# Giving VectorE's remainders of Q and K, the rounded parts' products and the adaLN columns another place in a hybrid attention layer's order of work

## The chip, the cores and the metric

The kernel runs on one core of a Trainium2 chip. The metric is the device time of one execution in microseconds, the lower the better. All matrix products are made in a rounded 32-bit type (float32r) with every operand split in two: a rounded part and the remainder that the rounding left. A product of two such operands takes three passes (rounded by rounded, rounded by remainder, remainder by rounded).

## The reference, cut to what matters

One layer of a streaming encoder is computed for 1024 rows of a prompt and 64 rows of a sample, with 1024 cached rows for the sample. `h` is a normalized and modulated `x` whose shift, scale and gate come from a product with `w_ada` (adaLN). Then:

```python
m = jax.nn.silu(c) @ w_ada[l] + b_ada[l]                  # shift1, scale1, gate1, shift2, scale2, gate2
qd, kd, vd, qs, ks, vs = split_proj(pre(h, g_pre_mix, shift1, scale1) @ w_in[l])
p = jax.nn.softmax(jnp.where(visible, qd kd^T * scale - alibi, NEG))       # 4 heads, two maps each
od = rmsnorm((p[0] - lam * p[1]) @ vd, subln_g) * (1 - lam_init)
w = jnp.where(earlier, jnp.exp(log_sigmoid(z) + between), 0)               # 8 heads, stick-breaking
osb = w @ vs
h = h + gate1 * rmsnorm(concat(od, osb) @ w_out, g_post_mix)
h = h + gate2 * rmsnorm(relu(pre(h, g_pre_ffn, shift2, scale2) @ w_up) ** 2 @ w_down, g_post_ffn)
```

K and V of both groups of heads are outputs too.

## The kernel before, in words

The head of the kernel loads a part of `w_ada`, turns its product into columns (A1, B1) and makes the transposed, split activations `hT` in three groups of columns (384, 384, and 256 of the prompt plus 64 of the sample). Then come eight units of 128 columns of Q, K and V: units 0 to 3 are the heads of differential attention, units 4 to 7 hold two stick-breaking heads each. After them come `w_out` and the second norm, and then the FFN in 16 blocks.

In the middle part two streams of work are written into each other. The main stream is a list of steps (`Diff`, `Stick`, `Sample`), each with `score` (products with K, exponentials or sigmoids) and `apply` (transposes, products with V). The second stream is a `Filler`: a first-in, first-out list of generators, in which each `yield` gives a cost. After each `yield` of the main stream, `fill.spend` runs the filler's generators until their costs have paid for the main stream's cost times a ratio, and `fill.until` drains what a step needs at once. The filler holds `proj(u, g)` for unit u and group g (in the order `proj_q`, `proj_k`, `proj_v`) at a cost of 12 each, and from unit 2 on one part of `rows` (the rows of gate1, then `modulation`, whose `ada_rows` and columns A2 and B2 the second norm needs).

`proj_q` makes 24 products of one PSUM bank `pq` (tag `pj`, two banks for all of the filler's work). Then, for each half of 64 partitions, ScalarE writes the rounded scaled copy (L488) and VectorE the remainder (L489), so that they are written as copy, remainder, copy, remainder. `proj_k` does it with one whole copy `kf` and two rounded copies in each half (L512, L513), and a remainder (L514). It then transposes `kf` and stores it (`natural`).

`apply` works in groups of up to four blocks of 128 by 128. A group is transposed into a PSUM bank, ScalarE rounds it (`ah`), VectorE takes the remainder (`al`, L65), and one group later `times` makes the products with V: for each block one with `ah` and one with `al` (L620 and L621 for Diff and Sample, L788 and L789 for Stick). All of a step's products add up in one bank `po`.

In `modulation`, VectorE copies the product's bank to `R` (L224), and two products with `sel` sum it into columns (L209). In the trace these tiles carry the names `Rm` and `pcm`.

The build plans the engines' orders itself: `TileContext(nc, schedule_with_timeline_sim=True)` is given the written order, and what the engines run is not the written order line for line. Semaphores are placed by it too. The engines are in order once it is built.

Of the kernel before, what the change touches and what calls it, by code (L numbers as in the profile page):

```python
# [16 lines left out]
P = 128  # L17
# [13 lines left out]
def fr(ap):  # L31
    return ap.bitcast(F32)


def build(tc, I, O):
# [17 lines left out]
    def brief(shape, name, tag, dt=F32, bufs=2):  # L53
        return atp.tile(shape, dt, tag=tag, name=name, bufs=bufs)

    def bank(name, tag):
        return pp.tile([P, 512], F32, tag=tag, name=name)

    load = nc.sync.dma_start
    mm = nc.tensor.matmul  # L60
# [60 lines left out]
    cc = brief([16, P], "cc", "o1", bufs=1)  # L121
# [83 lines left out]
    def sum_to_columns(R, n, name):  # L205

        ps = bank(name, "pj")
        for i in range(n):
            mm(ps[:, 2 * i : 2 * i + 2], lhsT=R[:, i * P : (i + 1) * P], rhs=sel, start=True, stop=True)  # L209
        return ps[:, 0 : 2 * n].rearrange("p (k j) -> p k j", j=2)  # L210

    def modulation(first, cols, name):

        A, B = (sb.tile([P, KT, 2], F32, name=x + name) for x in "AB")

        def gen():
            for q in range(4):
                ks = slice(2 * q, 2 * q + 2)
                for part in range(2):
                    nm = f"{name}{q}{part}"  # L220
                    c0 = first + D * part + 256 * q
                    ps = yield from ada_rows(c0, nm)
                    R = big("R" + nm, "s", [P, 512], F32)[:, :256]
                    nc.vector.tensor_copy(R, ps)  # L224
                    v = sum_to_columns(R, 2, "pc" + nm)
                    col = lambda c: cols[:, c : c + 2].unsqueeze(2).broadcast_to([P, 2, 2])
                    o = (B, A)[part][:, ks, :]
                    nc.vector.tensor_tensor(o, v, col(8 + (c0 - first) // P), ALU.add)
                    if part:
                        nc.vector.scalar_tensor_tensor(o, o, 1.0, col(2 * q), ALU.add, ALU.mult)  # L230
                    yield None

        return A, B, gen()
# [240 lines left out]
    def proj_q(u, g, wq):  # L474
        c0, n = GRP[g]
        qs = -0.125 if u < 4 else 0.125
        if g == 0:
            U[u]["Q"] = [big(f"Q{u}{m}", "qk", [P, TP]) for m in range(2)]
        Q = U[u]["Q"]
        if u + g:  # L480
            ps = bank(f"pq{u}{g}", "pj")
            yield from dense_T(ps, wq, hT, g)
        else:
            ps = PS[0]
        w = min(n, TP - c0)
        for m in range(2):
            r, o = slice(64 * m, 64 * m + 64), slice(64 - 64 * m, 128 - 64 * m)
            nc.scalar.mul(Q[m][r, c0 : c0 + w], ps[r, :w], qs)  # L488
            nc.vector.scalar_tensor_tensor(Q[m][o, c0 : c0 + w], ps[r, :w], qs, fr(Q[m][r, c0 : c0 + w]), ALU.mult, ALU.subtract)  # L489
        if g == 2:  # L490
            qsm = brief([P, TS], f"qsm{u}", "ms", bufs=1)
            nc.scalar.mul(qsm, ps[:, 256:320], qs)
            load(smD[u, :, 0, :], qsm)

    def proj_k(u, g, wk):
        c0, n = GRP[g]
        if g == 0:
            U[u]["Kd"] = [big(f"K{u}{m}", "qk", [P, TP]) for m in range(2)]
            U[u]["Kl"] = big(f"Kl{u}", "qk", [P, TP])
        Kd, Kl = U[u]["Kd"], U[u]["Kl"]  # L500
        if u + g:
            ps = bank(f"pk{u}{g}", "pj")
            yield from dense_T(ps, wk, hT, g)
        else:
            ps = PS[1]
        w = min(n, TP - c0)
        cols = slice(c0, c0 + w)
        kf = small([P, 384], f"kf{u}{g}", "kf", bufs=2)
        nc.scalar.copy(kf[:, :n], ps[:, :n])
        for m in range(2):  # L510
            r, o = slice(64 * m, 64 * m + 64), slice(64 - 64 * m, 128 - 64 * m)
            nc.scalar.copy(Kd[m][r, cols], ps[r, :w])  # L512
            nc.scalar.copy(Kd[m][o, cols], ps[r, :w])  # L513
            nc.vector.tensor_tensor(Kl[r, cols], ps[r, :w], fr(Kd[m][r, cols]), ALU.subtract)  # L514
        if g == 2:
            load(smD[u, :, 1, :], kf[:, 256:320])
        natural(kf, u, g, kout, f"k{u}{g}")
        yield 0.33
# [91 lines left out]
    def apply_rows(po, parts, values):  # L610

        n = sum(len(p[0]) for p in parts)
        done = 0
        pend = []

        def times(ah, al, blocks, kr):
            nonlocal done
            for i in range(len(blocks)):
                v = values(done)
                mm(po[:, 0:256], lhsT=ah[:kr, i * P : (i + 1) * P], rhs=v.rearrange("p a d -> p (a d)"), start=(done == 0), stop=False, skip_group_check=True)  # L620
                mm(po[:, 0:P], lhsT=al[:kr, i * P : (i + 1) * P], rhs=v[:, 0, :], start=False, stop=(done == n - 1), skip_group_check=True)  # L621
                done += 1

        for blocks, kr, name, pre in parts:
            if pre:
                pre()
            pend.append((*transposed(blocks, name, kr), blocks, kr))
            yield 0.11 * len(blocks)
            if len(pend) == 2:
                times(*pend.pop(0))  # L630
                yield 0.8
        yield 0.1
        while pend:
            times(*pend.pop(0))
            yield 0.8
# [111 lines left out]
    class Stick:  # L747
# [26 lines left out]
        def apply(self):  # L774
            u, q, hd = self.u, self.q, self.hd
            r, o = slice(64 * hd, 64 * hd + 64), slice(64 - 64 * hd, 128 - 64 * hd)
            V = U[u]["V"]
            po = bank(f"po{self.name}", "pv")
            pend = []

            def times(jp, ah, al):
                for i in range(2):
                    j = 2 * jp + i
                    v = V[:, j, hd, :]
                    lone = j == 2 * q + 1
                    out = po[:, P:256] if lone else po[:, 0:256]
                    cc = slice(256, 384) if lone else slice(256 * i, 256 * i + 256)
                    mm(out, lhsT=v, rhs=ah[:, cc], start=(j == 2 * q), stop=False, skip_group_check=True)  # L788
                    mm(out, lhsT=v, rhs=al[:, cc], start=False, stop=(j == 1), skip_group_check=True)  # L789

            for jp in reversed(range(q + 1)):
                blocks = [(j, t) for j in (2 * jp, 2 * jp + 1) for t in range(2) if not (j == 2 * q + 1 and t == 0)]
# [290 lines left out]
    for m in range(NTT):  # L1083
        g, off = m // 3, (m % 3) * P
# [28 lines left out]
        r = rstd(sumsq([p[:rows] for p in pss], rows, f"sso{m}", jk), rows, f"rso{m}")  # L1113
# [3 lines left out]
        r = rstd(sumsq([a[:rows] for a in x], rows, f"ssb{m}", jk), rows, f"rsb{m}")  # L1117
# [114 lines left out]
    for b in range(NB - 1):  # L1232
# [12 lines left out]
        if last:  # L1245
            GG2 = gate("g2", 1, "h")
            wd2 = [down_weights(b + 1, i, i == 0) for i in range(2)]
            done = []
# [57 lines left out]
```

## Time and profile before

| | us |
|---|---|
| median of 3 runs | 1553.53 (1546.62 to 1556.1) |
| the profiled execution's own time | 1554.56 |
| its span, from first to last instruction | 1552.7 |
| busy in the span: TensorE, its weight loads | 1499.0, 1341.8 |
| busy in the span: VectorE, ScalarE, GpSimd | 918.1, 700.1, 342.7 |

The span is cut below into the head (to 75 us), the eight units (75 to 600 us), the turn from the last unit to `w_out` (600 to 690 us), and the rest (from 690 us). A busy TensorE is not TensorE at its peak, since matmuls overlap and their ends are modelled; the distance from one matmul's start to the next tells its rate. In a view of waits a line reads: the waiting engine, its tile and line, who ended the wait, the total in us, the number of times, the longest.

### The profile page before, as it was taken

What the parts mean: (1) busy time and instruction counts of PE and PEld (TensorE: products, weight loads), DVE (VectorE), ACT (ScalarE), POOL (GpSimd) and SP (SyncE); (2) the same over time, 40 slices, a digit from 0 to 9 for tenths busy, and PEclk for the clock granted to TensorE, in tenths of its full rate; (3) what the DMA queues carried; (4) which work ended last, traced back from release to release, by engine and by line L of the source; (5) the groups of instructions that cost most, each with busy time, mean ns of one, the idle gap of its engine ahead of it and who ended that gap; (6) DMA issues with size and microseconds to landing.
All of it is one profiled execution on the core that took longest, in us unless ns stands there. A gap on an engine that the chain in (4) does not pass through costs nothing.

```text
span 1552.7 us, 23586 instructions
## 1 busy us (share of the span) xinstructions
PE 1499.0 (97%) x8714; PEld 1341.8 (86%) x8714; DVE 918.1 (59%) x1761; ACT 700.1 (45%) x1650; POOL 342.7 (22%) x519
## 2 busy tenths in 40 slices
PE   6899999989999999899999999999999999999998
PEld 4789898878899988778898988899989999899896
DVE  3776877675868687866442445454554544544447
ACT  3766766666768577837653112121122112121122
POOL 1453443434333333622110000000000000000002
PEclk9999999999999999999999999999999999999999
DMA  9322333424232325444221122211111111111025
GB/s 315 119 60 82 93 115 100 119 62 124 71 113 60 111 88 159 124 122 140 75 66 52 34 79 82 70 40 41 55 54 41 46 37 42 54 55 41 28 82 183
DMA packets 152517, 133.20 MB, mean 86 GB/s; under 512 B 11234, under 2 KB 136275, under 8 KB 152403
## 3 DMA queue, kind: packets, MB, share of 16 engines
q1 hardware_dynamic: 152402, 131.71, 27.6%
q8 instruction: 68, 1.11, 0.3%
q14 instruction: 47, 0.38, 0.1%
HBM read 108.59 MB, written 23.09 MB: 85 GB/s over the span
## 4 chain that ended last, share of the span: by engine, by line
PE 64%; issue 4%; ACT 4%; DVE 3%; POOL 1%; DMA 1%; SPq 0%; DVEq 0%; POOLq 0%; ACTq 0%
PE pu L303 8%; PE pu L305 8%; PE pu L304 8%; PE pd L1181 8%; PE pd L1182 8%; PE pd L1184 7%; PE py L1096 1%; PE py L1098 1%; PE pt L604 1%; PE py L1095 1%; PE po L789 1%; PE pq L303 1%; PE pq L305 1%; PE pq L304 1%; PE pk L303 1%
## 5 line engine op out<-in xcount | busy, mean ns | idle before, releaser
L1188 DVE TENSOR_TENSOR acc<-pd,acc 128x512 f32<-128x512 f32 x252 | 171.8, 687 | 113.6 <-PE pd L1184 107.8
L1166 ACT ACTIVATE sq<-pu 128x384 f32<-128x384 f32 (+1 forms) x96 | 45.1, 470 | 308.3 <-PE pu L305 308.3
L1167 DVE TENSOR_TENSOR sq<-sq 128x384 f32<-128x384 f32 (+1 forms) x96 | 72.1, 751 | 171.8 <-ACT sq L1166 171.8
L65 DVE TENSOR_TENSOR al<-pt,ah 128x512 fp32r<-128x512 f32 (+2 forms) x128 | 75.6, 598 | 19.1 <-ACT ah L64 17.7
L593 PE MATMUL pz<-K,Q 128*128 128x128 f32 (+2 forms) x192 | 72.9, 382 | 4.5 <-DVE mn L678 1.9
L64 ACT CAST ah<-pt 128x512 fp32r<-128x512 f32 (+2 forms) x128 | 65.9, 522 | 24.5 <-PE pt L604 16.7
L604 PE MATMUL pt<-ident,s 128*128 128x128 f32 x432 | 70.0, 277 | 4.2 <-DVE al L65 1.5
L642 ACT ACTIVATE s<-s,mn 128x512 f32<-128x512 f32 (+3 forms) x96 | 58.6, 611 | 23.3 <-DVE mn L678 19.7
L594 PE MATMUL pz<-Kl,qz 128*128 128x128 f32 (+2 forms) x192 | 66.6, 350 | 0.0
L740 DVE TENSOR_TENSOR_SCAN s<-k,s 128x128 f32<-128x128 f32 (+1 forms) x64 | 58.2, 922 | 11.4 <-POOL s L769 7.1
L604 PEld LDWEIGHTS pt<-ident,s 128*128 128x128 f32 x432 | 51.6, 141 | 9.2 <-DVE al L65 2.0
L65 DVE TENSOR_TENSOR rl<-sq,rh 128x384 fp32r<-128x384 f32 x64 | 35.7, 558 | 38.1 <-ACT rh L64 38.1
L442 POOL CAST qz<-Q 64x256 fp32r<-64x256 f32 x64 | 36.9, 576 | 90.5 <-PE pz L594 71.8
L764 ACT ACTIVATE s<-pz 128x128 f32<-128x128 f32 (+2 forms) x96 | 47.8, 498 | 15.5 <-PE pz L594 14.9
L64 ACT CAST rh<-sq 128x384 fp32r<-128x384 f32 x64 | 32.8, 513 | 40.2 <-DVE sq L1167 38.2
L765 ACT ACTIVATE k<-pz 128x128 f32<-128x128 f32 (+2 forms) x96 | 47.9, 499 | 0.0
L789 PE MATMUL po<-al,V 128*128 128x256 f32 (+1 forms) x160 | 41.4, 293 | 6.3 <-DVE al L65 6.3
L740 DVE TENSOR_TENSOR_SCAN s<-k,s,s 128x512 f32<-128x512 f32 x32 | 43.6, 1371 | 5.1 <-ACT k L765 5.1
L593 PEld LDWEIGHTS pz<-K,Q 128*128 128x128 f32 x192 | 36.6, 191 | 11.2 <-DVE mn L678 4.6
L678 DVE CUSTOM_DVE_ANT_0 s<-pz,T 128x512 f32<-128x512 f32 (+3 forms) x64 | 37.3, 585 | 12.4 <-PE pz L594 11.9
L788 PE MATMUL po<-ah,V 128*128 128x256 f32 (+1 forms) x160 | 43.8, 284 | 0.7 <-ACT ah L64 0.7
L64 ACT CAST r<-sq 128x320 fp32r<-128x320 f32 x32 | 14.8, 461 | 62.7 <-DVE sq L1167 62.7
(1232 smaller groups left out, 5125.5 us busy)
## 6 DMA issues: line engine op xcount, KB each, us to landing
arr<-in_w_ada SPq DMA_DIRECT2D x16, 512.0 KB
arm<-in_w_ada SPq DMA_DIRECT2D x16, 512.0 KB
ar<-in_w_ada SPq DMA_DIRECT2D x10, 512.0 KB
mixD<-mx SPq DMA_DIRECT2D x32, 128.0 KB
xr<-in_x_prompt SPq DMA_DIRECT2D x16, 256.0 KB
xD<-xr SPq DMA_DIRECT2D x16, 256.0 KB
xy<-xD SPq DMA_DIRECT2D x8, 512.0 KB
out_y_prompt<-xy SPq DMA_DIRECT2D x16, 256.0 KB
```

Of the source, the lines that this page charges most:

```text
L64: (eh or nc.scalar.copy)(hi, src)
L65: (el or nc.vector).tensor_tensor(lo, src, fr(hi), ALU.subtract)
L303: mm(ps[:, :n], lhsT=wh[:, k, :], rhs=hh[:, k, :n], start=(k == 0), stop=False)
L304: mm(ps[:, :n], lhsT=wh[:, k, :], rhs=hl[:, k, :n], start=False, stop=False)
L305: mm(ps[:, :n], lhsT=wl[:, k, :], rhs=hh[:, k, :n], start=False, stop=(k == 7))
L593: mm(ps[:, :w], lhsT=S["Q"][m][:, qt], rhs=S["Kd"][m][:, c0 : c0 + w], start=True, stop=False)
L604: nc.tensor.transpose(pt[:kr, i * P : (i + 1) * P], a, ident)
L740: nc.vector.tensor_tensor_scan(d, k, d, 0.0 if later is None else later[:, 0:1], ALU.mult, ALU.add)
L1181: mm(ps, lhsT=rh[:, off : off + P], rhs=wh[:, cols], start=(j == 0), stop=False)
L1182: mm(ps, lhsT=rh[:, off : off + P], rhs=wl[:, cols], start=False, stop=(m == 8 and end))
L1184: mm(ps, lhsT=rl[:, off : off + P], rhs=wh[:, cols], start=False, stop=end)
L1188: nc.vector.tensor_tensor(acc[m][:, cols], ps, acc[m][:, cols], ALU.add)
```

## The change

There are four edits. In `modulation` a `yield 0.2` stands between the copy to `R` and the products that sum it, so that other work may be written between them. In `proj_q` both copies are written first, then a `yield 0.2`, then both remainders. In `proj_k` all copies are written first, then a `yield 0.2`, then both remainders. In both, the break is left out for the first unit's first group. In the two functions `times`, all of a group's products with `ah` are written first, then all of its products with `al`.

```diff
@@ modulation
                     nc.vector.tensor_copy(R, ps)
+                    yield 0.2
                     v = sum_to_columns(R, 2, "pc" + nm)
@@ proj_q
-        for m in range(2):
-            r, o = slice(64 * m, 64 * m + 64), slice(64 - 64 * m, 128 - 64 * m)
+        rows_ = [(slice(64 * m, 64 * m + 64), slice(64 - 64 * m, 128 - 64 * m)) for m in range(2)]
+        for m, (r, o) in enumerate(rows_):
             nc.scalar.mul(Q[m][r, c0 : c0 + w], ps[r, :w], qs)
+        if u + g:
+            yield 0.2
+        for m, (r, o) in enumerate(rows_):
             nc.vector.scalar_tensor_tensor(Q[m][o, c0 : c0 + w], ps[r, :w], qs, fr(Q[m][r, c0 : c0 + w]), ALU.mult, ALU.subtract)
@@ proj_k
             nc.scalar.copy(Kd[m][r, cols], ps[r, :w])
             nc.scalar.copy(Kd[m][o, cols], ps[r, :w])
+        if u + g:
+            yield 0.2
+        for m in range(2):
+            r = slice(64 * m, 64 * m + 64)
             nc.vector.tensor_tensor(Kl[r, cols], ps[r, :w], fr(Kd[m][r, cols]), ALU.subtract)
@@ apply_rows
         def times(ah, al, blocks, kr):
             nonlocal done
-            for i in range(len(blocks)):
-                v = values(done)
-                mm(po[:, 0:256], lhsT=ah[:kr, i * P : (i + 1) * P], rhs=v.rearrange("p a d -> p (a d)"), start=(done == 0), stop=False, skip_group_check=True)
-                mm(po[:, 0:P], lhsT=al[:kr, i * P : (i + 1) * P], rhs=v[:, 0, :], start=False, stop=(done == n - 1), skip_group_check=True)
-                done += 1
+            vs = [values(done + i) for i in range(len(blocks))]
+            for i, v in enumerate(vs):
+                mm(po[:, 0:256], lhsT=ah[:kr, i * P : (i + 1) * P], rhs=v.rearrange("p a d -> p (a d)"), start=(done + i == 0), stop=False, skip_group_check=True)
+            for i, v in enumerate(vs):
+                mm(po[:, 0:P], lhsT=al[:kr, i * P : (i + 1) * P], rhs=v[:, 0, :], start=False, stop=(done + i == n - 1), skip_group_check=True)
+            done += len(blocks)
@@ Stick.apply
             def times(jp, ah, al):
-                for i in range(2):
-                    j = 2 * jp + i
-                    v = V[:, j, hd, :]
-                    lone = j == 2 * q + 1
-                    out = po[:, P:256] if lone else po[:, 0:256]
-                    cc = slice(256, 384) if lone else slice(256 * i, 256 * i + 256)
-                    mm(out, lhsT=v, rhs=ah[:, cc], start=(j == 2 * q), stop=False, skip_group_check=True)
-                    mm(out, lhsT=v, rhs=al[:, cc], start=False, stop=(j == 1), skip_group_check=True)
+                for a in (ah, al):
+                    for j in (2 * jp, 2 * jp + 1):
+                        lone = j == 2 * q + 1
+                        out = po[:, P:256] if lone else po[:, 0:256]
+                        c0 = 256 * (j % 2)
+                        mm(out, lhsT=V[:, j, hd, :], rhs=a[:, c0 : c0 + (P if lone else 256)], start=(a is ah and j == 2 * q),
+                           stop=(a is al and j == 1), skip_group_check=True)
```

## Rows read from the trace of the kernel before

**Rows 1.** Windows: length; PE, PEld, DVE, ACT, POOL busy (instructions); clock, DMA, GB/s.

```profile
0.00:75.00 75.00, 56.21 (x365) 42.37 (x366) 38.99 (x99) 43.46 (x108) 21.50 (x48) 0.91 0.69 222
75.00:600.00 525.00, 507.81 (x3423) 467.39 (x3424) 380.36 (x894) 358.48 (x953) 204.41 (x327) 1.00 0.31 92
600.00:690.00 90.00, 79.65 (x473) 68.32 (x472) 70.67 (x99) 59.65 (x128) 46.54 (x47) 0.94 0.47 145
690.00:1552.00 862.00, 855.31 (x4458) 763.67 (x4456) 428.08 (x671) 238.47 (x463) 70.29 (x98) 1.00 0.21 64
```

**Rows 2.** Waits of TensorE's matmuls, 75 to 690 us.

```profile
PE po L789 <- DVE al L65: 6.3, 9, 1.1
PE poS L621 <- DVE alS L65: 3.8, 2, 2.2
PE pcm L209 <- DVE Rm L224: 3.1, 4, 1.0
...
PE pz L593 <- DVE mn L678: 1.9, 5, 0.8
```

**Rows 3.** Waits of TensorE's weight loads, 75 to 690 us.

```profile
PEld po L789 <- DVE al L65: 8.9, 10, 1.3
...
PEld pcm L209 <- DVE Rm L224: 4.3, 4, 1.3
```

**Rows 4.** Timeline of TensorE, 581 to 585 us (start, us, what, idle before it).

```profile
581.56 0.28 PE L789 MATMUL po<-al,V 128*128 128x256 f32 x1
581.67 0.28 PE L788 MATMUL po<-ah,V 128*128 128x256 f32 x1
581.79 0.28 PE L789 MATMUL po<-al,V 128*128 128x256 f32 x1
...
583.53 0.61 PE L209 MATMUL pcm<-sel,Rm 128*128 128x2 f32 x4 [1.02 <-DVE Rm L224]
```

**Rows 5.** Timeline of TensorE, 260.9 to 261.2 us.

```profile
260.92 0.33 PE L620 MATMUL po<-V,ah 128*128 128x256 f32 x1
...
261.15 0.33 PE L620 MATMUL po<-V,ah 128*128 128x256 f32 x1
```

**Rows 6.** Timeline of TensorE, 624 to 625 and 674 to 678 us.

```profile
624.39 0.48 PE L621 MATMUL poS<-cv,alS 128*128 128x128 f32 x1 [1.57 <-DVE alS L65]
...
675.69 0.47 PE L621 MATMUL poS<-Vn,alS 64*128 64x128 f32 x1 [2.22 <-DVE alS L65]
```

**Rows 7.** Timeline of ScalarE, 112.5 to 116 us.

```profile
112.72 0.48 ACT L488 ACTIVATE Q<-pq 64x384 fp32r<-64x384 f32 x1 [1.50 <-PE pq L305]
113.82 0.49 ACT L488 ACTIVATE Q<-pq 64x384 fp32r<-64x384 f32 x1 [0.62 <-DVE Q L489]
```

**Rows 8.** Timeline of VectorE, 112.5 to 116 us.

```profile
113.24 0.55 DVE L489 SCALAR_TENSOR_TENSOR Q<-pq,Q 64x384 fp32r<-64x384 f32 x1 [2.34 <-ACT Q L488]
...
114.67 0.56 DVE L489 SCALAR_TENSOR_TENSOR Q<-pq,Q 64x384 fp32r<-64x384 f32 x1
```

**Rows 9.** Waits of VectorE, 75 to 690 us.

```profile
DVE Kl L514 <- ACT K L513: 16.5, 22, 2.8
...
DVE Q L489 <- ACT Q L488: 12.8, 12, 2.4
```

**Rows 10.** Waits of ScalarE, 75 to 690 us.

```profile
ACT K L512 <- DVE Kl L514: 5.7, 6, 2.2
...
ACT Q L488 <- DVE Q L489: 4.7, 7, 0.9
```

**Rows 11.** Timeline of ScalarE, 250 to 262 us.

```profile
255.39 0.47 ACT L513 CAST K<-pk 64x384 fp32r<-64x384 f32 x1
255.89 0.59 ACT L64 CAST ah<-pt 128x512 fp32r<-128x512 f32 x1
...
258.12 0.47 ACT L512 CAST K<-pk 64x384 fp32r<-64x384 f32 x1
```

**Rows 12.** Line L489, who waited for it (us, times).

```profile
  PEld pv L303: 0.3, 1
```

## The prediction

> **What bounds the kernel now.** I read the busy times by stage first. From 690 us on, TensorE is busy for 855.3 of 862 us at full clock [rows 1]; of the change's work only a few last products fall there, so at most the time at which this stage starts can move. The head (to 75 us) holds only the first group's projections, which skip the breaks, and the first of the second group's. What is left is the eight units and the turn to `w_out`, 75 to 690 us. In the units TensorE is idle for 525 - 507.8 = 17.2 us, in the turn for 90 - 79.7 = 10.3 us, at a mean granted clock of 0.94 there [rows 1]. So 27.5 us is all that any edit of waits can win, unless the clock comes back too: 0.06 of 90 us, or 5.4 us more. VectorE is busy for 72% of the units and ScalarE for 68%; neither bounds the stage, and both matter only where TensorE waits for them.
>
> The second view is who ended TensorE's waits in this stretch. The largest three are those the change aims at: the remainder products of Stick (6.3 us in nine waits), those of Sample (3.8 us in two) and the adaLN sums (3.1 us in four) [rows 2]. Behind them stand VectorE's score reductions with 1.9 us. The same waits seen at the weight loads, which start ahead of the matmul, are 8.9 and 4.3 us [rows 3]; I take these as the upper ends. The third view is the waits of VectorE and ScalarE around the copies of Q and K, and the fourth their order in time.
>
> **The columns.** The edit adds no instruction; the sums L209, the two or three small VectorE operations behind them and everything after them in the filler's list come later by 0.2 of pacing. In the trace TensorE stands before these sums because VectorE comes to the copy L224 late: at 583.53 us it had waited 1.02 us [rows 4]. There are eight such sums and four waited. With the break, main-stream work stands between. How much the planner puts there can't be read from this trace. The lower bound is zero (the planner may place the sums as before), the upper the whole 4.3 us [rows 3]. Below zero nothing is likely, since A2 and B2 are first read in the second norm, after 690 us. A wait is at most 1.3 us long and one block product takes 0.12 us [rows 4], so a few products fill only a part of it. I take **2.5 us gained**, nearer to the 3.1 us of the matmul's own rows.
>
> **Rounded products first.** First the rate. In Stick a product of 256 columns starts 0.11 to 0.12 us after the one before, whether both have the same V block or not (581.56 to 581.67 to 581.79 us, [rows 4]). In Diff a pair starts every 0.23 us [rows 5], which is two such steps. So the new order neither gains nor loses rate: zero, within 0.01 us for each of some 370 pairs, or 4 us either way. What it changes is a wait. A Stick group has two blocks; where TensorE stood for `al` after one product with `ah`, it can now do one more, 0.12 us. Nine waits by 0.12 is 1.1 us. Of the two Sample waits, the longer one (2.22 us at 675.69) doesn't gain: it is a product of 64 partitions, a group with a single block, which has no second rounded product to put ahead. The other (1.57 us at 624.39) is in a group of four blocks, so three products go ahead of it, 0.36 us [rows 6]. The upper end is all of 8.9 us [rows 3], if an `ah` that is read earlier lets ScalarE round the next group earlier; the lower end is zero. I take **1.5 us**, by these ten waits.
>
> **The remainders.** The trace shows what the written order costs. ScalarE's copy of the lower half of `pq` ends at 113.20 us, VectorE's remainder runs from 113.24 to 113.79, and only then, at 113.82, ScalarE copies the upper half, with 0.62 us idle ended by VectorE [rows 7, 8]. I found this order, the upper copy after the lower remainder has ended, in all 24 groups of Q and all 24 of K. For K it also lets other work slip in: the upper half's copies come at 258.12 us, 2.3 us after the lower half's [rows 11]. So a bank takes three handovers between the engines; with the copies written together it takes one.
>
> What that takes away: ScalarE's waits for a remainder, 5.7 + 4.7 = 10.4 us [rows 10], and about half of VectorE's waits for a copy, (16.5 + 12.8) / 2 = 14.7 us [rows 9]. The remaining half stays, because VectorE's first remainder now waits for both copies, 0.48 us later than before. Idle time of these two engines isn't the end of the path. VectorE's idle time in the units is 525 - 380.4 = 144.6 us [rows 1], and 14.7 us is a tenth of it. The named waits of TensorE for VectorE sum to 6.3 + 3.8 + 3.1 + 1.9 = 15.1 us [rows 2]; a tenth of them is **1.5 us**. The bounds are minus 1.1 us a group at worst (two remainders of 0.55 us late, [rows 8]) and plus 5 us.
>
> The Trainium skill (PSUM — Partial Sum Buffer, "PSUM bank collisions raise a hardware error") says that two engines may access one bank at the same time where they touch different quadrants of 32 partitions. By that rule the upper half's copy need not stand behind the lower half's remainder, the change would take none of ScalarE's handovers away, and I would estimate the term at nothing and the sum below at 4.0 us. The trace disagrees for this build: the copy stands behind the remainder every time, with idle time on its engine in 13 cases [rows 10].
>
> What the break moves along: behind Q's remainders the sample's `qsm` and its store, behind K's remainders the store of `kf`, its transposes and VectorE's copies, and their stores through SP's queue. They are stores, and the sample's K is read back a unit later; no row of TensorE's waits names them, so I set them to zero. The breaks also enter the pacing: 0.4 per `proj`, against costs of 12 filed and about 12.2 used in a full group (three times 3.84, and 0.33 for each of two or three yields). That is 3% of a group's pacing; it makes the units' last generators drain slightly more at their due time. Zero, as long as remainders aren't late (below).
>
> **The sum.** 2.5 + 1.5 + 1.5 = 5.5 us. Against the profiled execution, 1554.56 us (a span of 1552.7 and 1.86 around it), that gives 1549.06. That execution is 1.03 us above the median of 1553.53, so against the median the forecast is **1548.0 us**, 0.35% faster. A change of under 1%, 15.5 us, is about what a measurement of this kernel cannot tell from none: its three runs lie 9.5 us apart.
>
> **Rivals.** *The new order brings back no time.* The engines' order isn't the written one: between L513 of one half and L512 of the next, written side by side, ScalarE runs other work, a rounding of `pt` among it [rows 11]. The planner already puts ready work in front of work that isn't ready, by its own times; the waits are where the chip was later than planned. A break shifts them elsewhere. For it: the waits are scattered, nine of 0.7 us and four of 0.8 us, and each handover avoided needs a row behind it that is ready. Time: -2 to +4 us around 1553, by the rate bound above.
>
> *Much more comes back.* The turn from the last unit is VectorE's stretch (70.7 of 90 us busy), and TensorE's clock is down there [rows 1]. If shorter chains bring forward the last Stick steps, the turn's idle time of 10.3 us, the 5.4 us of clock, and some of the first waits go together: 15 us, or 1538.5. Against it: the long wait at 675.69 us [rows 6] isn't touched.
>
> *Slower: the remainders come too late.* Their place is the pair of `pj` banks. `pq` keeps its bank until both remainders are done, and the first product of the same group's `pv` needs that bank. In the trace this wait shows once, 0.3 us [rows 12]. VectorE takes work in the order built, so with a break, reductions of 0.7 us and scans stand in front of the remainders. It decides when the pair ends after the 24 products of `pk` and the steps between. Then a remainder pair of 1.1 us [rows 8] begins to show on TensorE. There are 46 breaks; if a third of each pair shows, it costs 46 x 0.37 = 17 us: 1570. Against it: 0.2 of pacing is less than a single step's yield, and the product runs of `pk` are long.
>
> **How the numbers follow.** The forecast (2 to 9 us faster) gets 0.48, no net gain 0.27, much more 0.13, slower by late banks 0.12. The range must reach into both outer cases: 1537 to 1560 leaves out about half of either, 0.12 together, and a little for a wider scatter of the new order. Faster by over 1% (below 1538.0) is half of the third case and a bit of scatter, 0.08; slower by over 1% (above 1569.1) is half of the last, 0.06; the rest, 0.86, is within 1%.
>
> **What would show it.** The columns: the wait of L209 for L224 falls from 3.1 to under 1.5 us. The products: L620s and L788s stand together, and the waits of L789 fall by about 1 us but don't vanish. The remainders: both L488 run back to back, ScalarE's waits for L489 and L514 are gone, VectorE's waits for a copy are half. Wrong would be: waits of L303 for L489 or L514 of several us (late banks); the same 27 us of TensorE's idle time under other names (nothing comes back); or the turn at full clock with under 5 us idle (much more).

## The result and the profile after

The change makes the kernel slower: a median of **1564.65 us** (6 runs, 1561.11 to 1566.89) against 1552.86 us for the kernel before (6 runs), a ratio of **1.0079** with a 95% interval of 1.0060 to 1.0098. The forecast was 1548.0 us with a range to 1560. The profiled execution's span is 1562.2 us, 9.5 us longer. All medians here are of fast runs; one run of `r3_remainders_11_6` (1724.5 us) and one of the kernel before beside `h1_halves` (1842.0 us) were slow ones and are left out.

The windows of the changed kernel, in the columns of [rows 1]:

```profile
0.00:75.00 75.00, 55.91 (x358) 40.98 (x358) 36.87 (x94) 41.02 (x103) 18.87 (x45) 0.98 0.68 222
75.00:600.00 525.00, 502.15 (x3359) 461.03 (x3358) 381.60 (x885) 354.66 (x941) 204.06 (x326) 0.99 0.31 92
600.00:690.00 90.00, 77.92 (x497) 68.42 (x495) 77.11 (x110) 65.04 (x142) 43.13 (x51) 0.98 0.42 132
690.00:1562.00 872.00, 864.85 (x4511) 771.68 (x4508) 430.80 (x678) 241.60 (x467) 69.77 (x98) 1.00 0.21 65
```

TensorE's idle time in the units is 525 - 502.15 = 22.9 us (17.2 before), in the turn 90 - 77.92 = 12.1 us (10.3 before). That is 34.9 us against 27.5: **7.4 us of the 9.5 are idle time between 75 and 690 us**. Another 0.8 us is idle time outside it, and TensorE is busy 1.8 us longer in all (1500.8 us against 1499.0). The last stage only starts later. (The three make 10.0 us because the windows end at whole microseconds.)

Who ended TensorE's waits in the changed kernel, 75 to 690 us (engine, line, waited for: us in total, times, longest), as in [rows 2]:

```profile
PE po L796 <- DVE al L65: 10.9, 8, 3.9
PE pnv L460 <- DVE mx L816: 4.5, 2, 2.4
PE pm L657 <- POOL od L720: 3.0, 1, 3.0
PE pz L601 <- DVE Q L493: 2.9, 1, 2.9
PE pz L601 <- DVE mn L687: 2.0, 5, 0.8
```

The two waits that the change aimed at most directly have left the list: the adaLN sums (3.1 us in [rows 2]) and Sample's remainder products (3.8 us). Stick's remainder products, which were to fall from 6.3 by 1.1 us, rose to 10.9; 9.6 of these lie in the turn. Two entries are new: `pnv` behind a mixing operation of VectorE, and `pz` behind Q's remainders. The wait of `pm` for GpSimd grew from 0.9 to 3.0 us.

The remainders of Q themselves, line L493 (idle time of VectorE before them by releaser, then who waited for them):

```profile
its engine sat idle before it (us, times) until:
  ACT Q L489: 12.9, 13
who waited for it (us, times):
  PEld pz L601: 3.1, 1
  PE pz L601: 2.9, 1
  ACT qsm L496: 0.3, 1
  PE pv L304: 0.2, 1
```

ScalarE's copies no longer wait for a remainder (4.7 us in [rows 10]), so the edit does what it says. VectorE's wait for the copies was to be halved and isn't: 12.9 us after 12.8 in [rows 9], and 14.7 us after 16.5 for K. The banks' wait that the slower rival spoke of is 0.2 us.

**The new wait for Q's remainders**, early in the units, shows what the order does. The timeline of the changed kernel, 98 to 102 us (start, us, engine, what, idle before it):

```profile
98.04 0.79 ACT L489 ACTIVATE Q<-pq 64x256 fp32r<-64x256 f32 x2
...
98.23 2.35 POOL L65 TENSOR_TENSOR wq1l<-wq1r,wq1h 128x1024 fp32r<-128x1024 f32 x1 [2.14 <-ACT wq1h L64]
...
99.39 1.21 DVE L697 SCALAR_TENSOR_TENSOR cf<-l,nlam,cf 128x1 f32<-128x1 f32 x1
...
100.63 0.87 DVE L493 SCALAR_TENSOR_TENSOR Q<-pq,Q 64x256 fp32r<-64x256 f32 x2
...
101.10 0.91 PE L601 MATMUL pz<-K,Q 128*128 128x512 f32 x2 [2.86 <-DVE Q L493]
```

Both copies are done at 98.83 us, but the two remainders start only at 100.63, behind other work of VectorE's queue (`cf` among it, which here takes 1.21 us in place of 0.22), and `score` of the first half waits 2.86 us for them. Before, half 0 was copied at 95.64 us with its remainder at 96.77, and half 1 at 100.06 with its remainder at 101.28: each shortly ahead of the score products that read it, and ScalarE did 4 us of other work between the two copies.

**The two waits of `pnv`** (2.05 and 2.43 us) have another cause. The same view, 481 to 486 us:

```profile
481.11 2.37 POOL L65 TENSOR_TENSOR wv6l<-wv6r,wv6h 128x1024 fp32r<-128x1024 f32 x1
...
481.74 3.78 DVE L749 TENSOR_TENSOR_SCAN s<-k,s,s 128x512 f32<-128x512 f32 x1
...
484.15 1.46 POOL L778 TENSOR_SCALAR_AFFINE_SELECT s<-s 128x128 f32<-128x128 f32 x2
...
485.44 0.39 DVE L816 TENSOR_TENSOR mx<-po,ot 64x256 f32<-64x256 f32 x1
```

A scan whose median is 1.28 us takes 3.78 us. It begins while GpSimd subtracts `wv6l`; two short subtractions (`df`) follow there, and the scan ends 1.33 us after the last of them, about a scan's own time. The operation that `pnv` needs is queued behind it. At 561.92 us the same happens with 4.17 us. At 99.39 us it was `cf`, 1.21 us where its median is 0.22, that ends 20 ns after GpSimd's `wq1l`.

The two longest waits, both for `al` in the turn (3.85 us at 643.35 and 2.99 at 679.79), have such operations ahead of them in VectorE's queue too: a `sod` of 1.95 us for 0.22 beside `wo2l`, then an `skt` of 2.13 for 0.29 and an `sst` of 2.25 for 0.22 beside `wo4l` and `wo5l`. I added up what VectorE's operations took over the median of their kind, where this was more than a quarter and 0.15 us: from 60 to 700 us it is 19 us before and 32 us after.

### The profile page after: what moved, and what is told of

Same layout as the page of the kernel before. It is cut to its first block, busy times and chain, and to the rows that moved or that the text cites. A ratio compares the mean times of both kernels' runs of the same rounds, so it can differ in the third digit from the quotient of the medians.

```text
span 1562.2 us, 23607 instructions
## 1 busy us (share of the span) xinstructions
PE 1500.8 (96%) x8717; PEld 1342.1 (86%) x8717; DVE 926.4 (59%) x1764; ACT 702.3 (45%) x1651; POOL 335.8 (21%) x520
## 4 chain that ended last, share of the span: by engine, by line
PE 81%; ACT 5%; issue 5%; DVE 4%; DMA 3%; POOL 1%; SPq 1%; DVEq 0%; POOLq 0%; ACTq 0%
PE pu L304 8%; PE pu L306 8%; PE pu L305 8%; PE pd L1189 8%; PE pd L1190 8%; PE pd L1192 7%; PE pt L612 2%; PE pq L304 2%; PE pq L305 2%; PE pq L306 2%; PE pk L304 2%; PE pk L305 2%; PE pk L306 2%; PE pz L601 2%; PE pz L602 2%
## 5 line engine op out<-in xcount | busy, mean ns | idle before, releaser
L64 ACT CAST ah<-pt 128x512 fp32r<-128x512 f32 (+2 forms) x128 | 65.8, 522 | 37.3 <-PE pt L612 16.6
L749 DVE TENSOR_TENSOR_SCAN s<-k,s 128x128 f32<-128x128 f32 (+1 forms) x64 | 60.1, 955 | 12.3 <-POOL s L778 6.8
L773 ACT ACTIVATE s<-pz 128x128 f32<-128x128 f32 (+2 forms) x96 | 48.1, 501 | 24.3 <-PE pz L602 23.6
L749 DVE TENSOR_TENSOR_SCAN s<-k,s,s 128x512 f32<-128x512 f32 x32 | 50.2, 1574 | 5.2 <-ACT k L774 4.7
L778 POOL TENSOR_SCALAR_AFFINE_SELECT s<-s 128x128 f32<-128x128 f32 x64 | 31.8, 503 | 80.1 <-ACT s L773 68.1
L443 POOL CAST qz<-Q 64x256 fp32r<-64x256 f32 x64 | 30.0, 468 | 81.8 <-PE pz L602 70.2
L796 PE MATMUL po<-al,V 128*128 128x256 f32 (+1 forms) x160 | 33.3, 290 | 11.0 <-DVE al L65 10.9
```

Source lines behind the costliest of these rows:

```text
L64: (eh or nc.scalar.copy)(hi, src)
L749: nc.vector.tensor_tensor_scan(d, k, d, 0.0 if later is None else later[:, 0:1], ALU.mult, ALU.add)
```

## The experiments

My theory was that the new order itself costs: it makes the first half's operands late and puts ScalarE's copies in one block. The first rival ("scatter" in the expectations) is that the order of the whole middle part is drawn anew by any edit, and that the one before was a good draw; the second ("lock"), that VectorE's operations stretched by GpSimd's make the loss.

All ratios are against the kernel before, timed beside each on the same chip. "Idle" is TensorE's idle time from 75 to 690 us, worked out from two window rows as above (before 27.5, after 34.9); the clocks are those of the units and of the turn in the same rows (before 1.00 and 0.94, after 0.99 and 0.98). Both belong to the one profiled execution, which can lie some us off the median (1561.85 us in `k2_Q_alone`, 1561.94 in `r3_remainders_11_6`, 1552.42 in `d1_pieces_before`).

| run | kernel | us | ratio, 95% interval | idle, us | clocks |
|---|---|---|---|---|---|
| c1_columns | columns' break alone | 1561.5 | 1.0066 (1.0041 to 1.0092) | 28.9 | .99 .92 |
| c2_products | products' order alone | 1555.6 | 1.0027 (1.0010 to 1.0045) | 27.8 | 1.00 .96 |
| c3_remainders | both projections' edits alone | 1560.5 | 1.0054 (1.0036 to 1.0072) | 28.0 | .98 .96 |
| c4_order_alone | the same without breaks | 1567.2 | 1.0098 (1.0067 to 1.0129) | 34.4 | .99 .96 |
| n1_before_12_4 | before, cost 12.4 | 1559.8 | 1.0053 (1.0034 to 1.0073) | 31.8 | .99 .94 |
| n2_before_11_6 | before, cost 11.6 | 1551.0 | 0.9988 (0.9974 to 1.0003) | 23.6 | .99 .96 |
| m1_after_12_4 | after, cost 12.4 | 1568.9 | 1.0110 (1.0088 to 1.0131) | 36.6 | .98 .94 |
| m2_after_11_6 | after, cost 11.6 | 1560.9 | 1.0057 (1.0035 to 1.0079) | 31.4 | .98 .96 |
| k1_K_alone | K's edit alone | 1573.5 | 1.0134 (1.0101 to 1.0166) | 34.4 | .98 .96 |
| k2_Q_alone | Q's edit alone | 1558.1 | 1.0044 (1.0024 to 1.0064) | 31.5 | .98 .96 |
| r1_columns_11_6 | columns, cost 11.6 | 1556.5 | 1.0022 (1.0004 to 1.0039) | 26.7 | .98 .96 |
| r3_remainders_11_6 | projections, cost 11.6 | 1555.2 | 1.0028 (1.0007 to 1.0049) | 30.2 | .97 .96 |
| d1_pieces_before | before, GpSimd cut | 1555.1 | 1.0024 (1.0002 to 1.0047) | 24.3 | .99 .94 |
| d2_pieces_after | after, GpSimd cut | 1561.4 | 1.0062 (1.0042 to 1.0081) | 29.9 | .98 1.00 |
| x5_K_parted | K's edit, block parted | 1562.2 | 1.0064 (1.0044 to 1.0084) | 30.2 | .98 .96 |
| x6_whole_without_K | whole change but K's edit | 1566.0 | 1.0090 (1.0059 to 1.0122) | 33.7 | .98 .96 |
| h1_halves | old order with breaks | 1574.9 | 1.0148 (1.0129 to 1.0166) | 37.3 | .98 .94 |
| v1_cut_11_6 | before, cost 11.6, GpSimd cut | 1547.7 | 0.9973 (0.9964 to 0.9982) | 23.4 | .99 1.00 |

Idle time alone doesn't carry these times: `c1_columns`, `c3_remainders`, `r1_columns_11_6` and `x5_K_parted` have -0.8 to 2.7 us more of it than the kernel before, and profiled spans 2.6 to 10.5 us longer. Most of the rest goes with the clock. From 75 us to shortly before the end, TensorE ran at the lower of its two levels (1.2 GHz in place of 2.4) for 13.7 us before, 17.1 after, 27.3 in these four, 34.1 in `k1_K_alone` and 37.5 in `h1_halves`. If half of that time is lost (my estimate), idle time and clock together give each span's distance from the one before to within 5.4 us (`after`: 7.4 + 1.7 = 9.1 of 9.5). In the changed kernel the clock fell at four of the long waits: it is 1.00 from 95 to 100 us and 0.66 from 100 to 105, around the wait for Q's remainders, and falls likewise at 347, 487 and 644 us. So a wait costs more than its own length.

**The parts.** Each takes its hunks of the diff above alone; `c4_order_alone` is `c3_remainders` without its two breaks:

```diff
-        if u + g:
-            yield 0.2
```

> Only the break ahead of adaLN's sums. Three theories are on trial for the changed kernel's 12 us loss. Lock: VectorE's operations whose operands all lie in SBUF (the scans above all) end only when a GpSimd remainder that ran beside them ends, and the new order makes them meet more often: operations of VectorE that last over 1.25 times their kind's median plus 0.15 us cost 32 us of excess after, 20 us before. Late remainders: the break puts Q's and K's remainders behind other work, and the next step waits for them. Scatter: any small change of the written order gives another plan, and plans differ by some 10 us either way. Lock and late remainders: this one stays within 4 us of before, with an excess of about 20 us; the sums' wait of 3.1 us falls. Scatter: it may well move by 5 us or more, either way.

> Only the products with the rounded parts first. Lock and late remainders: within 4 us of before, the waits for al a little shorter than 6.3 us. Scatter: it may move by 5 us or more either way.

> Only proj_q and proj_k, with their breaks. Late remainders: slower by 8 to 14 us, with waits of TensorE for L489 and L514's successors of several us. Lock: slower by 6 to 14 us with an excess of VectorE's stretched operations near 32 us, and few waits for the remainders themselves. Scatter: anything from -8 to +14 us.

> proj_q and proj_k with the copies together and the remainders right behind, without the break. Late remainders: no loss, 0 to 4 us faster than before, as nothing is put in front of the remainders. Lock: it follows the excess of stretched operations, 0.6 us of time for 1 us of excess over 20. Scatter: it differs from the run with the breaks by 5 us or more in no set direction.

No part gains: 8.9, 3.0 and 7.9 us lost (against 1552.58 beside them), 19.8 together where the whole loses 11.8. So the parts don't add up, and each redraws what stands beside it. The copies together without a break lose 14.6 us: the new order loses without its breaks too. The columns' waits show a gain given back. TensorE's waits in `c1_columns`, 75 to 690 us:

```profile
PE po L790 <- DVE al L65: 5.8, 5, 2.1
PE poS L622 <- DVE alS L65: 5.2, 2, 3.0
PE pdv L552 <- POOL df L541: 2.3, 2, 1.3
PE pz L594 <- ACT k L766: 2.0, 3, 1.0
...
PE pnv L460 <- DVE mx L809: 1.3, 1, 1.3
```

The sums' wait, 3.1 us in [rows 2], is down to 1.2, as forecast. But Sample's waits grew from 3.8 to 5.2 us, waits for `k` and `mx` are new, and the clock of the turn is 0.92. In `c2_products` Stick's waits rose to 8.2 us in ten and Sample's to 5.1 in two.

**Another pacing.** One number of the filler, in the kernel before and after:

```diff
-                fill.add(proj(u, g), 12, (u, g))
+                fill.add(proj(u, g), 12.4, (u, g))      # or 11.6
```

> The kernel before with nothing of the change: only the cost filed for a projection in the pacing is 12.4 in place of 12, so that the main stream and the projections are written into each other a little differently. Each of the four parts of the change, run alone, was slower (by 9, 3, 8 and 15 us), and they don't add up to the whole's 12. Scatter: the kernel before stands at a lucky plan, and this one, too, lands slower by 3 to 15 us (1556 to 1568). If the change's own edits are at fault: within 3 us of before (1550 to 1556).

> The same with 11.6. Scatter: 1556 to 1568, and not the same as with 12.4. Own edits at fault: 1550 to 1556.

> The changed kernel with a filed cost of 12.4. Scatter: the changed kernel's 1564.65 is one draw of the same pot, so this lands anywhere from 1553 to 1570, and the mean of changed kernels is that of the unchanged ones paced the same, within 4 us. Own edits at fault: it stays at 1562 to 1568, some 12 us above its unchanged partner with 12.4.

> The changed kernel with a filed cost of 11.6. Scatter: 1553 to 1570. Own edits at fault: 1562 to 1568, some 12 us above its unchanged partner with 11.6.

A cost of 12.4 alone, with no edit, loses 6.6 us, and 11.6 moves the time by -2.2 us, which is within the noise: a plan drawn anew can be worth more than the whole forecast gain. The change loses at each pacing nonetheless: 11.8 us at 12, 1568.88 - 1559.8 = 9.1 at 12.4, 1560.92 - 1550.98 = 9.9 at 11.6.

**K and Q apart, and two parts at 11.6.** K's edit or Q's alone; then columns or projections with the lower cost.

> Only proj_k's new order with its break; proj_q, columns and products as before. With three pacings the changed kernel is 9 to 12 us slower than its unchanged partner, so the edits themselves cost something. Theory block: ScalarE's five copies of K, 0.47 us each, now stand in one block of 2.4 us where the bank's hand-over used to part them, and roundings (ah), exponentials and copies to mx that TensorE needs queue behind it: K alone is then 4 to 8 us slower, and TensorE's waits for ScalarE behind such a block show. Theory late Q: the loss lies with Q's remainders alone (one wait of TensorE of 2.9 us near 100 us, one of 1.5 near 67): K alone is within 2 us of before.

> Only proj_q's new order with its break. Late Q: slower by 5 to 9 us, with TensorE's wait for L489's successor of about 3 us near 100 us, half of the clock beside it, and the 1.5 us wait near 67 us. Block: within 3 us of before, since Q's two copies make a block of 1 us only.

> The columns' break alone at a filed cost of 11.6, partner of the unchanged kernel at 11.6 (1551.0) as the one at 12 (1561.5) is of before (1552.6). If the break itself costs the 9 us, this is near 1560. If that was the luck of one plan, this differs from its partner by another amount, -4 to +5 us: 1547 to 1556.

> The remainders' edit alone at a filed cost of 11.6. If it costs the 8 us by itself, as the stalls of the first 330 us say that stand in all five kernels that hold it (10 to 17 us of stalls there against 6 to 9), this is at 1557 to 1561. If luck, 1547 to 1556.

K's edit alone loses 21.4 us, more than either theory had expected, Q's alone 6.0, both 7.9 (`c3_remainders`). At 11.6 the columns lose 5.5 us and the projections 4.2 against `n2_before_11_6` (timed on another chip): less than at 12, but not zero. Q's edit carries the wait near 100 us with it: `pz` stands 2.4 us for Q's remainders in `k2_Q_alone`, 2.8 in `c3_remainders`, 2.4 in `c4_order_alone`, and no such wait is in the kernel before. In all nine kernels with Q's edit it is 1.9 to 2.9 us, in the eleven without at most 0.6. What K's edit does is to be seen on ScalarE, in `k1_K_alone`, 214 to 224 us:

```profile
217.54 0.47 ACT L509 COPY kf<-pk 128x384 f32<-128x384 f32 x1
217.91 0.47 ACT L512 CAST K<-pk 64x384 fp32r<-64x384 f32 x1
218.39 0.47 ACT L513 CAST K<-pk 64x384 fp32r<-64x384 f32 x1
218.87 0.47 ACT L512 CAST K<-pk 64x384 fp32r<-64x384 f32 x1
219.36 0.48 ACT L513 CAST K<-pk 64x384 fp32r<-64x384 f32 x1
219.86 0.48 ACT L64 CAST V<-pnv 128x384 fp32r<-128x384 f32 x1
220.24 0.48 ACT L535 COPY vf<-pv 128x384 f32<-128x384 f32 x1
220.61 0.60 ACT L64 CAST ah<-pt 128x512 fp32r<-128x512 f32 x1
```

Five copies stand in one block of 2.3 us where the old order let a rounding between the halves [rows 11]. Such a block stands in 18 of 23 groups here and in 2 before. `V`, `vf` and `ah` queue behind it, and TensorE's waits in the same kernel, 110 to 330 us, name what ScalarE makes:

```profile
PE pzS L871 <- ACT bd L64: 3.0, 1, 3.0
PE par L201 <- ACT vf L535: 1.6, 1, 1.6
PE pgr L245 <- ACT ah L64: 1.5, 1, 1.5
```

None of these is in the kernel before in that stretch. But only the one for `vf`, at 220.77 us, stands right behind such a block. The wait for `ah`, at 271.36, comes some 6 us after its block, with exponentials between. The longest, for `bd` at 297.68, isn't ScalarE's at all; it had stood idle for the sample's K, which is read back through memory:

```profile
296.81 0.24 ACT L64 CAST Kn<-kn 128x64 fp32r<-128x64 f32 x1 [3.60 <-DMA kn<-smD]
```

In `m1_after_12_4` the same wait is 3.1 us.

**GpSimd's long operations cut, K's block parted, the change without K.** In the first two, the 128x1024 remainders of weights on GpSimd are made in four pieces; `x5_K_parted` moves K's break into the loop of copies (a break behind each half's two), and `x6_whole_without_K` leaves `proj_k` as it was:

```diff
+        step = shape[1] // 4
+        for i in range(4):
+            c = slice(step * i, step * i + step)
+            nc.gpsimd.tensor_tensor(lo[:, c], raw[:, c], fr(hi[:, c]), ALU.subtract)
```

> The kernel before with GpSimd's remainder of each weight block (128 x 1024, 2.4 us) cut into four of 128 x 256; nothing of the change. VectorE's operations on SBUF that run beside such a remainder end only when it ends (one of a column of 128 x 1 that took 1.6 us in place of 0.16, scans of 3.3 us in place of 1.3), 20 to 38 us of excess in each kernel so far. Lock: the excess falls from 22 to under 14 us, and the time by 2 to 8 us, to 1545 to 1551, since the turn's waits behind stretched scans (1.6 and 2.2 us) go. Lock beside the point: the excess falls, the time stays within 1550 to 1562 by the plan's own scatter.

> The same on the changed kernel. Lock as the cause of the loss: its excess falls from 33 to under 16 us and the time comes to within 4 us of the other cut kernel. Block (ScalarE's copies of K in a row, Q's first remainder behind both copies): it stays 7 to 14 us above the other cut kernel, with 6 us or more of stalls to 110 us and over 4 us from 110 to 330 us.

> K alone, as in the run that was 21 us slower, but with a break of 0.2 behind each half's two copies, so that ScalarE's five copies don't stand in one block. Block: TensorE's waits from 110 to 330 us that end with ScalarE work queued behind K's copies are gone, stalls there fall from 8.6 us to under 4, and the time falls by at least 8 us of the 21, to 1553 to 1565. If the remainders' lateness is the cause: no better than the run with one break, 1568 or more.

> The whole change with proj_k left as before: columns, products and Q's edit. Block: stalls from 110 to 330 us are back under 4 us as in all seven kernels without K's edit (the seven with it: 4.2 to 10.4), and the time is 3 to 8 us below the changed kernel's 1564.65. Scatter: anything from 1553 to 1572, and the stalls of that stretch may stand at either.

The changed kernel with the cut is 3.2 us faster (1564.65 to 1561.42, in two comparisons whose intervals overlap), with `pnv`'s waits down from 4.5 to 2.3 us and the longest scan from 4.17 to 2.75; on the kernel before the cut cost 3.1. The stretching fell as expected in both, from 19 to 13 us and from 32 to 16, so less of it isn't in itself less time. The loss at equal GpSimd work is still 1561.42 - 1555.12 = 6.3 us.

`x5_K_parted` doesn't test the block, since its break didn't part it in the engines' order. ScalarE, 217 to 220 us:

```profile
217.11 0.48 ACT L509 COPY kf<-pk 128x384 f32<-128x384 f32 x1 [0.35 <-DVE Vn L65]
217.49 0.47 ACT L512 CAST K<-pk 64x384 fp32r<-64x384 f32 x1
217.97 0.47 ACT L513 CAST K<-pk 64x384 fp32r<-64x384 f32 x1
218.45 0.48 ACT L512 CAST K<-pk 64x384 fp32r<-64x384 f32 x1
218.94 0.48 ACT L513 CAST K<-pk 64x384 fp32r<-64x384 f32 x1
```

The five copies stand together in 18 of 23 groups, as in `k1_K_alone`. Yet the three waits above are gone and the loss of K's edit is halved, 21.4 to 10.1 us. So the block by itself makes neither those waits nor the 21 us; the two kernels differ as two plans do. Nor is K's edit the cause of the whole change's loss: without it that still loses 14.0 us, with over 6 us of waits from 110 to 330 us where under 4 were expected. Its largest entry is `pnv` for `mx`, 6.5 us in four waits.

**Breaks in the old order, and a candidate.** `h1_halves` keeps copy and remainder of a half together and adds a break behind each half; `v1_cut_11_6` joins the lower cost and the cut on the kernel before, whose written order it keeps.

```diff
             nc.vector.scalar_tensor_tensor(Q[m][o, c0 : c0 + w], ps[r, :w], qs, fr(Q[m][r, c0 : c0 + w]), ALU.mult, ALU.subtract)
+            if u + g:
+                yield 0.2
...
             nc.vector.tensor_tensor(Kl[r, cols], ps[r, :w], fr(Kd[m][r, cols]), ALU.subtract)
+            if u + g:
+                yield 0.2
```

> The kernel before with its old order kept in both projections (a half's copy, then the same half's remainder) and a break of 0.2 us of given-out work behind each remainder. Theory 1, the order is what costs: half 0's operands are ready as early as before, so TensorE's stalls from 60 to 110 us stay at 3.2 to 5.8 us, as in the kernels that leave Q alone, and those from 110 to 330 us at 1.1 to 3.5; the time is within 4 us of the kernel before (1549 to 1557). Rival, any break in these two places costs, since it moves ScalarE's and GpSimd's given-out work and the plan with it: 6 to 14 us slower (1558 to 1566), with the old order and the head's stalls unchanged.

> The kernel before with the filler's cost at 11.6 and GpSimd's 128x1024 weight remainders cut in four. If what the shorter GpSimd operations take off VectorE's stretched ones and what the lower pacing gives add up, 1546 to 1551, faster than both kernels. If each is only another plan, drawn anew: 1550 to 1558, no gain.

My theory that the order is what costs falls as stated: the old order with breaks is the slowest kernel of all, 23.2 us behind the one beside it, and slower than the rival had it too. Its waits, 75 to 690 us, have in part yet other names:

```profile
PE po L793 <- DVE al L65: 4.2, 3, 1.5
PE pz L597 <- DVE mn L682: 3.3, 6, 0.8
PE pm L652 <- POOL od L715: 3.2, 2, 2.5
PE pt L608 <- DVE s L704: 2.4, 2, 1.7
PE pm L652 <- DVE mn L682: 2.2, 1, 2.2
...
PE pq L303 <- DVE Kl L516: 1.7, 1, 1.7
```

Here a bank's wait for K's remainder does show (1.7 us, the prediction's third rival), and VectorE's score reductions come second, behind Stick's remainder products. `v1_cut_11_6` is faster than both kernels: 1547.66 us, 0.27% below the kernel before. Its windows:

```profile
75.00:600.00 525.00, 509.10 (x3424) 469.20 (x3423) 375.07 (x892) 359.16 (x952) 214.83 (x389) 0.99 0.31 92
600.00:690.00 90.00, 82.55 (x514) 70.92 (x513) 72.08 (x107) 62.91 (x136) 52.00 (x74) 1.00 0.51 156
```

The turn has full clock and 7.5 us idle. Alone, the cut stands at 1.0024 and the lower cost at 0.9988, which don't add up to 0.9973. Whether it is the two edits or a good draw, one kernel can't tell.

## Why the prediction was wrong

**The step that failed is the same in all three terms**: each counted the waits that its edit takes away as time won, with a lower end of zero for the columns and the products, and set what moves along with the edit to zero. Alone, the three measured losses of 8.9, 3.0 and 7.9 us for forecast gains of 2.5, 1.5 and 1.5. What stood in place of the gains were waits at other places, longer stretches at the lower clock, and an order that is laid out anew. The prediction put the breaks' 0.4 in the pacing at zero as well; a filed cost higher by 0.4 lost 6.6 us with no edit at all. It isn't this shift alone, though: filing 12.4 in the changed kernel, which makes up for the breaks' 0.4, gave 1568.9 us and not less.

**The remainders' term** (plus 1.5) is where the working itself was wrong. Its lower bound of minus 1.1 us a group I left to the rival of the late banks. It took a share of idle time that ends at VectorE and ScalarE for a share of TensorE's waits. I followed each group from the end of the last product of `pq` (or `pk`) to the ends of its remainders, in the rows of both timelines, and took means over the 23 groups behind the first:

| mean, us | Q first half | Q both | K first half | K both |
|---|---|---|---|---|
| before | 1.84 | 3.97 | 3.12 | 5.58 |
| after | 2.26 | 2.79 | 5.31 | 5.88 |

For Q both halves are ready 1.2 us sooner and the first 0.4 us later. For K the first is 2.2 us later, and both are no sooner. (Without the break, in `c4_order_alone`, they are at 2.36 and 2.95 us for Q, 4.52 and 5.05 for K: the removed handovers bring K's end 0.5 us forward, and the break takes this back.) What the new order takes is the early first half. The prediction had the first remainder 0.48 us late, which holds for Q and not for K, and gave it no price. It also set the sample's K, which is read back, to zero; in `k1_K_alone` and `m1_after_12_4` TensorE stood 3.0 and 3.1 us behind it. Measured, the two projections' edits lose 7.9 us at a cost of 12 and 1555.2 - 1550.98 = 4.2 us at 11.6 (kernels of two comparisons).

**The columns' term** (plus 2.5) was right about its wait (3.1 to 1.2 us in `c1_columns`, and off the list in the changed kernel) and wrong that a wait removed is time won: `c1_columns` loses 8.9 us, `r1_columns_11_6` 5.5 against `n2_before_11_6` (two comparisons). Something else was late next, at `poS` and `pz`; idle time grew by only 1.4 us, but the time at the lower clock doubled, 13.7 to 27.3 us.

**The products' term** (plus 1.5): rate as forecast. Stick's products in the changed kernel, 590 to 595 us:

```profile
590.51 0.42 PE L796 MATMUL po<-ah,V 128*128 128x256 f32 x2
590.77 0.40 PE L796 MATMUL po<-al,V 128*128 128x256 f32 x2
```

Two products start 0.26 us ahead of the next two, about the 0.11 to 0.12 us each of [rows 4]; the median step between Stick's products is 0.12 us in both kernels. The wait was to fall by one product each time and rose instead, in `c2_products` from 6.3 to 8.2 us. It loses 3.0 us, 1.0027 (1.0010 to 1.0045).

**The rivals.** No net gain, with "idle time under other names", is what each trace looks like, but I gave it at most 4 us of loss; the tell-tale I named for it was 27 us of idle time, and there were 34.9. The slower rival had the sign right and the mechanism wrong: in the changed kernel no row of L304 waits over 0.5 us for a remainder (0.2 for Q's at `pv`, 0.5 for K's at `pq`).

**What is shown and what stays open.** The whole change costs: at four equal settings (costs 12, 12.4, 11.6, and GpSimd cut) the loss is 11.8, 9.1, 9.9 and 6.3 us, 9.3 in the mean, and the fastest of these changed kernels (1560.9) is slower than the slowest unchanged one (1559.8). Shown with rows is one wait that Q's edit makes each time, 1.9 to 2.9 us for Q's remainders; in the changed kernel it is 2.86 us, with the clock falling beside it. Shown as well is that stretched scans stand ahead of `pnv`'s 4.5 us of waits, which the cut halves. K's block on ScalarE is not shown as a cause: it stands in `x5_K_parted` as in `k1_K_alone`, without the waits. These pieces don't add up to the loss in every kernel; `h1_halves` has neither block nor new order.

The twelve kernels that touch a projection in any way take 1555.2 to 1574.9 us, 1564.5 in the mean; the eight that don't, 1547.7 to 1561.5, 1555.0 in the mean. This isn't evidence for the written order of before, since `h1_halves`, the slowest of the twelve, has it. How much of the difference is a plan that had been fitted to these costs, and how much the later operands, stays open; a kernel in which the same order is kept while only one copy moves wasn't tried.

## What to carry to other kernels

Idle time that two helper engines spend handing a tile to and fro is no price until a wait of the bounding engine names it; ask which operand is needed first, since writing two halves together makes the first one late (here by 0.4 us for Q and 2.2 for K). Look in the trace whether an edit's order reached the engines before reading its time. Where a planner lays out the whole order from costs, time an edit at two or three pacings before believing a gain or loss of under 1%: here a change of 12 to 12.4 in one cost moved the time by 6.6 us. A wait that a local edit removes is won only where the next one is known, and time at the lower clock belongs beside idle time in the account.

## What the runs showed of the hardware

A VectorE operation with two operands in SBUF is held by a GpSimd subtraction of two SBUF operands that runs beside it, and the profile shows this as a longer operation, not as a wait. Of 31 such operations that began, in the traces of before and after, while a 128x1024 subtraction still had 0.3 us or more to run (60 to 690 us), 28 took over a quarter and 0.15 us longer than the median of their kind. None of 94 that read PSUM did, and none of the six reciprocals, which have one operand. Beside GpSimd's operations with one operand (selections, casts, scalings) none of 31 did. The summary of line L697 of the changed kernel (duration in ns min/median/max):

```profile
L697 DVE SCALAR_TENSOR_TENSOR cf<-l,nlam,cf x32: 202/219/1547, 64.7 to 349.7; 128x1 f32<-128x1 f32 x32
```

and that of the 128x512 scans, line L749:

```profile
L749 DVE TENSOR_TENSOR_SCAN s<-k,s,s x32: 1251/1280/4170, 403.0 to 687.8; 128x512 f32<-128x512 f32 x32
```

An operation on 128 single numbers took up to 1.55 us for 0.22. In the kernel before the sum `l` (L644), as small, takes 1.66 us at 239.06, beside a remainder of 2.39 us that began on GpSimd at 238.32. The Trainium skill (SBUF — State Buffer, "SBUF: two separate sides") says that a VectorE operation with two SBUF inputs and a GpSimd operation that reads SBUF share a port pair, which the one that starts first holds for its whole instruction while the other is blocked. The trace agrees for GpSimd's operations with two operands, and shows no such hold by those with one. The price here is that a scan of 1.28 us became one of 3.78 to 4.17 us in front of work that TensorE waited for.
